# Dilated attention in one kernel of two blocks: query tiles by halves of classes, one product with the values per four tiles, and a gather moved to GpSimd

## The chip, the cores and the metric

The kernel runs as one launch on one core of a Trainium2 chip. The metric is the device time of that launch in microseconds (us), as the median of several runs. TensorE (PE in the profile, its weight loads PEld), VectorE (DVE), ScalarE (ACT), GpSimd (POOL) and SyncE (SP, which issues all DMAs) each work through a queue of their own in order and wait for one another by semaphores.

## The reference

Two transformer blocks on 1024 tokens of width 1024, float32. The change lies in the second block's dilated attention alone: eight heads of 64, each a mixture of three patterns (window 128 with dilation 1, 512 with 4, 2048 with 16). Cut to what matters:

```python
DIL_PATTERNS = ((128, 1), (512, 4), (2048, 16))

def dilated_branch(q, k, v, slopes, window, dilation):
    # query t attends to t + j*dilation for j in [-r, r], r = window // (2*dilation)
    ...
    s = jnp.einsum('bqnche,bnkche->bnchqk', qs, kw).astype(jnp.float32) * scale + bias
    s = jnp.where(mask, s, MASK_VALUE)
    m = jnp.max(s, axis=-1, keepdims=True)
    e = jnp.exp(s - m)
    l = jnp.sum(e, axis=-1, keepdims=True)
    o = jnp.einsum('bnchqk,bnkche->bnqche', e.astype(v.dtype), vw)
    ...

def dilated_attention(q, k, v, slopes):
    for window, dilation in DIL_PATTERNS:
        o, lse = dilated_branch(q, k, v, slopes, window, dilation)
        ...
    w = jax.nn.softmax(jnp.stack(lses, axis=0), axis=0)
    return jnp.sum(w[..., None] * jnp.stack(outs, axis=0), axis=0)
```

The kernel computes the three patterns as one softmax: the table `tab` holds slope times distance minus the logarithm of how many patterns contain the pair.

## The kernel before

Eight head pairs follow one another in the second block, four of the differential attention and then four of the dilated one (here pairs 0 to 3, two heads each; `dil_attend`). Tokens are sorted by their residue modulo 4, so there are four classes of 256 tokens. A query tile is half a class, 128 queries; tile `i` is half `i % 2` of class `i // 2`. A tile sees five blocks of 128 keys and, at the edge of its window, 16 more keys from each of three classes, together 688 scores per query and head.

Each tile has three steps, and `pipeline` sets their order:

```python
yield A(0)
yield A(1)
for i in range(n):
    if i + 2 < n:
        yield A(i + 2)
    if i + 2 == n:
        yield None
    if i:
        yield C(i - 1)
    yield B(i)
yield C(n - 1)
```

- A (scores): for each head four matmuls into two PSUM banks (L1267, L1269), two reductions on VectorE that add the table and take the minimum (L1272), the exponential on ScalarE (L1275). The result is `N`, 128 x 688.
- B (transposes): VectorE collects the 3 x 16 more keys of each head into `more` (L1290); eleven transposes on TensorE (four and four in L1294, one of each head in L1300, `more` in L1301); four copies out of PSUM, which the helper `evac` gives to ScalarE (L630) and VectorE (L632) by turns. So the first head's four blocks go to ScalarE, the second's to VectorE, and of the third bank the two single blocks go to ScalarE and the more keys to VectorE (the narrow copy, 96 x 128).
- C (product with the values): ten matmuls with 64 weight columns, one per block and head, and 128 columns of data (L1318), and one for the more keys of both heads (L1319). The output bank is filled by four tiles and then copied by ScalarE (L1322).

`bank()` takes the next of eight PSUM banks; `slot()` takes one of 40 general SBUF buffers. While the tiles of a pair run, `merge` puts pieces of the next pair's key projection between the steps, by cost numbers that each step returns (A 1160, B 1199, C 1561) and the ratio 0.27895. At the `None` the tiles pause, the projection runs to its end, and the remaining steps C(5), B(6), C(6), B(7), C(7) are the five `t` in a string that orders the way to the next pair:

```python
"fqfqqqtNftNtfvNvtvtNveNzzzzx"
```

`q`, `v` and `z` are half pieces of projections (twelve matmuls of 512 columns, L112 to L114), `N` the steps of the norms of the next keys and queries (sums over heads L255, their transposes L264, a reciprocal square root in thirteen small VectorE operations up to L246, rows out by a transpose L271 and by DMA), `f` and `e` the finish of an earlier pair (L1148, L1158 on VectorE, `rows_out` L271). For the last pair there is no next one: GpSimd splits rows of the next weight (`wo`, L118 and L121), ScalarE and GpSimd split the finished outputs (`yt`, L120 and L121), and after C(6) `pair_last` needs the sums of all eight tiles (L1380 on VectorE, L271 on TensorE) before B(7) and C(7).

Of the kernel before, what the change touches and what calls it, by code (L numbers as in the profile page):

```python
# [9 lines left out]
F32 = mybir.dt.float32  # L10
# [3 lines left out]
AF = mybir.ActivationFunctionType  # L14
# [52 lines left out]
class Kern:  # L67
# [593 lines left out]
    def ssd_chunks(self, g, st):  # L661
        nc, te, V, G = self.nc, self.nc.tensor, self.nc.vector, self.nc.gpsimd
# [42 lines left out]
        def prep(c):  # L705
            c0 = 16 + 128 * c
            cols = slice(c0, c0 + 128)
            ab = self.slot("ab", w=1024)
            nc.sync.dma_start(out=ab, in_=self.d_acs[c, hs].rearrange("h l -> (h l)").partition_broadcast(128))
            xdt, xdd, bt = tokens(c + 1, c0, 128)  # L710
            ps = self.bank()
            te.matmul(ps[:, :128], st["B"][:, cols], st["C"][:, cols])
            cbm = self.sm.tile([128, 128], F32, tag="cbm", name="cbm", bufs=2)
            V.tensor_tensor(out=cbm, in0=self.U, in1=ps[:, :128], op=ALU.mult)
            E = self.ph.tile([128, 520], F32, tag="E", name="E", bufs=2)
            for e in range(2):
# [12 lines left out]
            return ab, E, xdt, xdd, bt  # L729
# [520 lines left out]
    def dil_attend(self, p, st):  # L1250
        nc, te, V = self.nc, self.nc.tensor, self.nc.vector
        bias, k = st["bias"], st["k"]
        y = st["y"] = self.slot("yb", w=T)
        Ns, PTs, O = {}, {}, [None]

        def A(i):
            d = dil_tile(i)
            own = d["own"]
            n0, n1 = own.stop - own.start, d["nrest"]
            Ns[i] = []  # L1260
            for j in range(2):
                N = self.slot("N", w=T)
                mn = self.sm.tile([128, 3], F32, tag="mn", name="mn", bufs=4)
                S = self.bank(), self.bank()
                q = st["q"][j][:, i * 128:(i + 1) * 128]
# [9 lines left out]
                nc.scalar.activation(out=N[:, :688], in_=N[:, :688], func=AF.Exp, scale=-1.0, bias=mn[:, 1:2],  # L1275
                                     accum_out=self.lall[:, 4 + 2 * p + j, i:i + 1])
                Ns[i].append(N)
            return 8 * 145

        def B(i):  # L1280
            d = dil_tile(i)
            if i == 0:
                st["vx"] = next(st["vx"])
            big, small = self.slot("pt", w=1024), self.slot("pt", w=512)
            more = self.sm.tile([128, 128], F32, tag="cbm", name="more", bufs=2)[:, :96]
            for j in range(2):
                N = Ns[i][j]
                x = N[:, 256:688] if d["a"] == 0 else N[:, 0:432]
                e = slice(128, 144) if d["a"] == 0 else slice(0, 16)
                V.tensor_copy(out=more[:, 48 * j:48 * j + 48].rearrange("p (c e) -> p c e", e=16),  # L1290
                              in_=x.rearrange("p (c e) -> p c e", e=144)[:, :, e])
                ps = self.bank()
                for b, (_, c) in enumerate(d["blocks"][:4]):
                    te.transpose(ps[:, b * 128:(b + 1) * 128], N[:, c:c + 128], self.ident)  # L1294
                self.evac(big[:, j * 512:(j + 1) * 512], ps)
                ps = None
            ps = self.bank()
            c = d["blocks"][4][1]
            for j in range(2):
                te.transpose(ps[:, j * 128:(j + 1) * 128], Ns[i][j][:, c:c + 128], self.ident)  # L1300
            te.transpose(ps[:96, 256:384], more, self.ident)  # L1301
            self.evac(small[:, :256], ps[:, :256])
            self.evac(small[:96, 256:384], ps[:96, 256:384])
            PTs[i] = big, small
            del Ns[i]
            return 11 * 109

        def C(i):
            d = dil_tile(i)
            big, small = PTs.pop(i)  # L1310
            if i % 4 == 0:
                O[0] = self.bank()
            q = slice((i % 4) * 128, (i % 4 + 1) * 128)
            for b in range(5):
                for j in range(2):
                    c = slice(64 * j, 64 * j + 64)
                    x = big[:, j * 512 + b * 128:j * 512 + (b + 1) * 128] if b < 4 else small[:, j * 128:(j + 1) * 128]
                    te.matmul(O[0][c, q], st["v"][:, d["blocks"][b][0], c], x, start=b == 0, stop=False)  # L1318
            te.matmul(O[0][:, q], st["vx"][:96, i * 128:(i + 1) * 128], small[:96, 256:384], start=False, stop=True)  # L1319
            if i % 4 == 3:  # L1320
                g = i // 4
                nc.scalar.activation(out=by_class(y)[:, 2 * g:2 * g + 2], in_=O[0].rearrange("p (r s) -> p r s", r=2),  # L1322
                                     func=AF.Copy)
            return 5 * 269 + 216

        yield from self.pipeline(8, A, B, C)

# [486 lines left out]
```

## Time and profile before

| | |
|---|---|
| time, median of 3 runs (lowest to highest) | 2732.16 us (2728.64 to 2733.09) |
| the profiled execution: its time, its span | 2729.51 us, 2727.7 us |
| busy over the span: PE, PEld | 2659.8 us (98%), 2232.2 us (82%) |
| busy over the span: DVE, ACT, POOL | 1372.3 us, 1165.6 us, 684.5 us |
| mean granted TensorE clock | 0.994 of full speed |
| dilated stage, 2194 to 2513 us: PE, DVE, ACT, POOL busy | 294.5, 170.7, 159.7, 75.1 of 319 us |

The span is the time from the first to the last instruction; the execution's own time is 1.8 us longer. Busy times are sums over instructions. Those of PE are modelled to each matmul's end and overlap, so from one matmul's start to the next one's is the better measure of its price. A clock of 1.00 is the upper of TensorE's two levels (2.4 GHz), 0.50 the lower (1.2 GHz).

### The profile page before, as it was taken

To read this page: it belongs to the slowest core of one execution; us is meant where nothing else is said; L and a number is where in the kernel's file an instruction comes from. 1 tells how busy PE (TensorE), PEld (TensorE's weight loads), DVE (VectorE), ACT (ScalarE), POOL (GpSimd) and SP (SyncE) were. 2 spreads that over 40 slices of the span, in tenths; PEclk is the share of its full clock that TensorE was granted. 3 is DMA by queue.
4 is the path that set the end of the run, shared out by engine and by line. 5 is a ranking of instruction groups with operands and counts; after the bars stand their busy time and mean duration, and the time that the engine had idled before them with its cause. 6 is when DMAs were issued, how large, how long until landed. Compare 5 with 4: busy or idle time off the path is not lost. (4 is left out here: it accounts for less than half of the span.)

```text
span 2727.7 us, 38674 instructions
## 1 busy us (share of the span) xinstructions
PE 2659.8 (98%) x14925; PEld 2232.2 (82%) x14925; DVE 1372.3 (50%) x2761; ACT 1165.6 (43%) x2080; POOL 684.5 (25%) x764
## 2 busy tenths in 40 slices
PE   8999999999999999999999999999999999998999
PEld 6888888888989889889877887878877877777877
DVE  5433322233574573654756777444654555446332
ACT  5554444445343433443432123445644555445331
POOL 1112121111243342342432333111111121204321
PEclk9999999999999999999999999999999999998999
DMA  3122222221123123122168653340222223324422
GB/s 131 58 64 72 78 79 71 78 64 62 39 88 114 55 78 116 55 103 91 55 207 279 205 182 131 128 121 30 72 70 70 79 94 94 86 72 146 160 65 70
DMA packets 85464, 266.87 MB, mean 98 GB/s; under 512 B 10880, under 2 KB 12032, under 8 KB 84256
## 3 DMA queue, kind: packets, MB, share of 16 engines
q1 hardware_dynamic: 85280, 264.40, 30.3%
q8 instruction: 117, 1.92, 0.3%
q14 instruction: 67, 0.55, 0.1%
HBM read 205.57 MB, written 33.49 MB: 88 GB/s over the span
## 5 line engine op out<-in xcount | busy, mean ns | idle before, releaser
L121 POOL TENSOR_TENSOR wlo<-wraw,whi 128x1024 fp32r<-128x1024 f32 (+2 forms) x168 | 374.4, 2232 | 1288.7 <-ACT whi L120 1077.8
L112 PE MATMUL bank<-uh,whi 128*128 128x512 f32 (+4 forms) x1752 | 625.8, 357 | 0.1
L114 PE MATMUL bank<-uh,wlo 128*128 128x512 f32 (+4 forms) x1752 | 618.8, 353 | 0.1
L113 PE MATMUL bank<-ul,whi 128*128 128x512 f32 (+4 forms) x1752 | 618.5, 353 | 0.0
L114 PEld LDWEIGHTS bank<-uh,wlo 128*128 128x128 f32 (+1 forms) x1752 | 327.9, 187 | 35.4 <-POOL wlo L121 0.5
L112 PEld LDWEIGHTS bank<-uh,whi 128*128 128x128 f32 (+1 forms) x1752 | 328.3, 187 | 34.3 <-issue 1.1
L113 PEld LDWEIGHTS bank<-ul,whi 128*128 128x128 f32 (+1 forms) x1752 | 328.2, 187 | 32.3
L112 PE MATMUL bank<-u,whi 128*128 128x512 f32 x512 | 207.8, 406 | 0.7 <-ACT pr L935 0.7
L113 PE MATMUL bank<-u,whi 128*128 128x512 f32 x512 | 203.6, 398 | 0.0
L114 PE MATMUL bank<-u,wlo 128*128 128x512 f32 x512 | 203.3, 397 | 0.0
L120 ACT ACTIVATE whi<-wraw 128x1024 fp32r<-128x1024 f32 (+2 forms) x169 | 155.3, 926 | 20.5 <-DMA wraw<-in_w_pa_dram 18.2
L630 ACT ACTIVATE pt<-bank 128x512 f32<-128x512 f32 (+1 forms) x320 | 143.0, 509 | 44.8 <-PE bank L624 38.1
L114 PE MATMUL bank<-yh,wlo 128*128 128x512 f32 x384 | 152.5, 397 | 1.0 <-POOL wlo L121 0.8
L112 PE MATMUL bank<-yh,whi 128*128 128x512 f32 x384 | 152.3, 397 | 0.9 <-ACT whi L120 0.9
L113 PE MATMUL bank<-yl,whi 128*128 128x512 f32 x384 | 151.9, 395 | 0.0
L647 DVE SCALAR_TENSOR_TENSOR acc<-raw,cwh,acc 128x1040 f32<-128x1040 f32 x72 | 93.7, 1302 | 109.5 <-ACT acc L644 107.8
L573 ACT ACTIVATE N<-N,mn 128x272 f32<-128x272 f32 (+7 forms) x128 | 100.3, 786 | 45.2 <-DVE mn L570 44.0
L114 PEld LDWEIGHTS bank<-u,wlo 128*128 128x128 f32 x512 | 97.2, 190 | 23.2
L112 PEld LDWEIGHTS bank<-u,whi 128*128 128x128 f32 x512 | 97.8, 191 | 22.3 <-ACT pr L935 1.1
L113 PEld LDWEIGHTS bank<-u,whi 128*128 128x128 f32 x512 | 97.6, 191 | 20.7
L121 POOL TENSOR_TENSOR wo<-wl,wo 128x512 fp32r<-128x512 f32 x52 | 73.4, 1425 | 157.8 <-ACT wo L120 150.6
L624 PE MATMUL bank<-cm,N 128*128 128x128 f32 x832 | 106.9, 273 | 0.0
(326 smaller groups left out, 4961.5 us busy)
## 6 DMA issues: line engine op xcount, KB each, us to landing
wraw<-in_w_in_dram SPq DMA_DIRECT2D x120, 512.0 KB, 4.1
gt<-d_gate SPq DMA_DIRECT2D x48, 512.0 KB, 5.7
ab<-d_acs SPq DMA_DIRECT2D x32, 512.0 KB, 3.5
qs<-qt SPq DMA_DIRECT2D x48, 256.0 KB, 2.9
wl<-in_w_out_dram SPq DMA_DIRECT2D x48, 256.0 KB, 5.4
tab<-in_tab_dram SPq DMA_DIRECT2D x8, 1056.0 KB, 5.9
cb<-d_csp SPq DMA_DIRECT2D x16, 520.0 KB, 7.6
d_gate<-gt SPq DMA_DIRECT2D x16, 512.0 KB, 2.9
```

The costliest lines, as they stand in the source:

```text
L112: te.matmul(ps, lh, rh, start=start, stop=False)
L113: te.matmul(ps, lh, rl, start=False, stop=False)
L114: te.matmul(ps, ll, rh, start=False, stop=stop)
L120: self.nc.scalar.activation(out=hi, in_=src, func=AF.Copy)
L121: (self.nc.vector if vector else self.nc.gpsimd).tensor_tensor(out=lo, in0=src, in1=hi.bitcast(F32), op=ALU.subtract)
L573: nc.scalar.activation(out=N[:, :W], in_=N[:, :W], func=AF.Exp, scale=-1.0, bias=mn[:, n - 1:n], accum_out=self.lall[:, 2 * p + j, i:i + 1])
L624: nc.tensor.transpose(ps[:, b * 128:(b + 1) * 128], N[:, c:c + 128], self.ident)
L630: self.nc.scalar.activation(out=out, in_=ps, func=AF.Copy)
L647: V.scalar_tensor_tensor(out=acc[:, :L], in0=raw[:, k:k + L], scalar=w(k), in1=acc[:, :L], op0=ALU.mult, op1=ALU.add)
```

## The change

- The tiles run in the order 0, 2, 4, 6, 1, 3, 5, 7: first the first halves of all classes, then the second halves. The four tiles of a group share four blocks of keys (the same half of every class); each has one block of its own besides (the other half of its class).
- C does nothing for three tiles and then the product of four: eight matmuls of 512 columns of data, eight of 128 for the own blocks, and eight of 128 for the more keys, now per head with 64 weight columns. The output bank is taken only there. C returns 0 or 5300 as its cost.
- The transposed blocks of a group stand in two tiles of 4 x 512 (`pt`), one for each head, with two general buffers beside them.
- The more keys are gathered by GpSimd at the end of A (L1283) in place of VectorE in B (L1290); their buffers go from two to four.

```diff
-            cbm = self.sm.tile([128, 128], F32, tag="cbm", name="cbm", bufs=2)
+            cbm = self.sm.tile([128, 128], F32, tag="cbm", name="cbm", bufs=4)
...
+        order = [0, 2, 4, 6, 1, 3, 5, 7]
         def A(i):
-            d = dil_tile(i)
+            t, d = order[i], dil_tile(order[i])
...
+            Xs[i] = self.sm.tile([128, 128], F32, tag="cbm", name="more", bufs=4)[:, :96]
...
+                nc.gpsimd.tensor_copy(out=Xs[i][:, 48 * j:48 * j + 48].rearrange("p (c e) -> p c e", e=16),
+                                      in_=x.rearrange("p (c e) -> p c e", e=144)[:, :, e])
             return 8 * 145
         def B(i):
...
-            big, small = self.slot("pt", w=1024), self.slot("pt", w=512)
+            if r == 0:
+                PTs[a] = ([self.ph.tile([128, 4, 512], F32, tag="pt", name="pt", bufs=2) for _ in range(2)],
+                          self.slot("pt", w=1024), self.slot("pt", w=512))
+            pt, own, more = PTs[a]
+            q = slice(128 * r, 128 * r + 128)
+            blocks = sorted(d["blocks"], key=lambda x: (x[0] % 2 != a, x[0]))
             for j in range(2):
-                V.tensor_copy(out=more[:, 48 * j:48 * j + 48].rearrange("p (c e) -> p c e", e=16),
-                              in_=x.rearrange("p (c e) -> p c e", e=144)[:, :, e])
...
-                self.evac(big[:, j * 512:(j + 1) * 512], ps)
+                self.evac(pt[j][:, :, q], ps.rearrange("p (b c) -> p b c", c=128))
...
-            self.evac(small[:, :256], ps[:, :256])
-            self.evac(small[:96, 256:384], ps[:96, 256:384])
+            self.evac(own.rearrange("p (j c) -> p j c", j=2)[:, :, q], ps[:, :256].rearrange("p (j c) -> p j c", j=2))
+            self.evac(more[:96, q], ps[:96, 256:384])
         def C(i):
...
-            for b in range(5):
-                for j in range(2):
-                    te.matmul(O[0][c, q], st["v"][:, d["blocks"][b][0], c], x, start=b == 0, stop=False)
-            te.matmul(O[0][:, q], st["vx"][:96, i * 128:(i + 1) * 128], small[:96, 256:384], start=False, stop=True)
...
-            return 5 * 269 + 216
+            if i % 4 != 3:
+                return 0
+            a = order[i] % 2
+            pt, own, more = PTs.pop(a)
+            O = self.bank()
+            for c in range(4):
+                for j in range(2):
+                    te.matmul(O[h], st["v"][:, 2 * c + a, h], pt[j][:, c], start=c == 0, stop=False)
+            for r in range(4):
+                for j in range(2):
+                    te.matmul(O[h, q], st["v"][:, 2 * r + 1 - a, h], own[:, j * 512 + 128 * r:j * 512 + 128 * r + 128],
+                              start=False, stop=False)
+            for r in range(4):
+                for j in range(2):
+                    te.matmul(O[64 * j:64 * j + 64, q], st["vx"][:96, t * 128 + 64 * j:t * 128 + 64 * j + 64], more[:96, q],
+                              start=False, stop=r == 3)
+            nc.scalar.activation(out=by_class(y)[:, :, 128 * a:128 * a + 128], in_=O.rearrange("p (r s) -> p r s", r=4),
+                                 func=AF.Copy)
+            return 5300
```

Three places show how the queues change. First TensorE, the norms on the way from pair 1 to pair 2 (`sums` are the sums over heads, `u` and `whi` a projection). Before:

```order
L1301 MATMUL bank<-cm,more 96x128
L264 MATMUL bank<-cm,sums_20281 128x128 x4
L1318 MATMUL bank<-pt_20283,vtok_19710 64x128 x8
L1318 MATMUL bank<-pt_20284,vtok_19710 64x128 x2
L1319 MATMUL bank<-pt_20284,vx_19837 128x128
L112 MATMUL bank<-u_1111_15416,whi_20205 128x512
```

With the change:

```order
L255 MATMUL bank<-qr_20122,w_152 32x512 x2
L1303 MATMUL bank<-cm,N_19979 128x128 x4
L1303 MATMUL bank<-cm,N_19991 128x128 x4
L1309 MATMUL bank<-cm,N_19979 128x128
L1309 MATMUL bank<-cm,N_19991 128x128
L1310 MATMUL bank<-cm,more 96x128
L264 MATMUL bank<-cm,sums_20192 128x128 x4
L112 MATMUL bank<-u_1111_15416,whi_20127 128x512
```

The product C(6) has gone from between the sums' transposes L264 and the half piece of projection after which L271 stands; C(5) has gone from before L255 likewise.

Second VectorE in pair 1, around the finish of pair 0 (L1158, `yb` is pair 0's output). Before:

```order
L1272 ISA N_19941,mn<-tab,bank,mn 128x288
L1272 ISA mn 128x1
L1158 TENSOR_TENSOR yb_18891<-yb_18891,rb_19636 128x4x256
L1290 COPY more<-N_19815 128x48
L1290 COPY more<-N_19826 128x48
L632 COPY pt_19979<-bank 128x512
L632 COPY pt_19980<-bank 96x128
L1272 ISA N_20002,mn<-tab,bank 128x400
```

With the change:

```order
L1275 ISA N_19889,mn<-tab,bank,mn 128x432
L1275 ISA mn 128x1
L632 COPY pt<-bank 128x4x128
L632 COPY pt_19814<-bank 96x128
L1158 TENSOR_TENSOR yb_18891<-yb_18891,rb_19588 128x4x256
L1275 ISA N_19936,mn<-tab,bank 128x400
```

It stood behind the reductions of A(4) and ahead of the copies of B(1); now it stands behind the copies of B(2) and ahead of the reductions of A(5).

Third TensorE at the end of pair 3 (`lall` are the sums of all tiles, `yt` and `wo` the product that follows the attention). Before:

```order
L1318 MATMUL bank<-pt_21857,vtok_21344 64x128 x8
L1318 MATMUL bank<-pt_21858,vtok_21344 64x128 x2
L1319 MATMUL bank<-pt_21858,vx_21464 128x128
L271 MATMUL bank<-cm,lall 16x128
L1294 MATMUL bank<-cm,N_21763 128x128 x4
L1294 MATMUL bank<-cm,N_21774 128x128 x4
L1300 MATMUL bank<-cm,N_21763 128x128
L1300 MATMUL bank<-cm,N_21774 128x128
L1301 MATMUL bank<-cm,more 96x128
L1318 MATMUL bank<-pt_21900,vtok_21344 64x128 x8
L1318 MATMUL bank<-pt_21901,vtok_21344 64x128 x2
L1319 MATMUL bank<-pt_21901,vx_21464 128x128
```

With the change:

```order
L1310 MATMUL bank<-cm,more 96x128
L271 MATMUL bank<-cm,lall 16x128
L1303 MATMUL bank<-cm,N_21599 128x128 x4
L1303 MATMUL bank<-cm,N_21611 128x128 x4
L1309 MATMUL bank<-cm,N_21599 128x128
L1309 MATMUL bank<-cm,N_21611 128x128
L1310 MATMUL bank<-cm,more 96x128
L1325 MATMUL bank<-pt,vtok_21200 64x512 x8
L1330 MATMUL bank<-pt_21578,vtok_21200 64x128 x8
L1336 MATMUL bank<-pt_21579,vx_21329 64x128 x8
```

The product ahead of L271 has gone, and the one at the end is that of four tiles.

## Rows read from the trace of the kernel before

**Rows 1.** Windows, the dilated stage: length; busy us (instructions) of PE, PEld, DVE, ACT, POOL; clock.
```profile
2194.00:2513.00 319.00, 294.49 (x1995) 245.35 (x1996) 170.73 (x476) 159.72 (x283) 75.11 (x116) 0.96 0.30 91
```

**Rows 2.** Groups by line, dilated stage: count, busy us, mean ns, idle before.
```profile
L1290 DVE COPY more<-N 128x48 f32<-128x48 f32 x64 | 9.7, 193 | 0.0
...
L1301 PE MATMUL bank<-cm,more 128*96 128x128 f32 x32 | 9.1, 286 | 9.9 <-DVE more L1290 9.9
```

**Rows 3.** Timeline of DVE and of ACT, one tile's step in pair 3.
```profile
2478.10 0.56 DVE L1272 CUSTOM_DVE_ANT_0 N<-tab,bank 128x400 f32<-128x400 f32 x1
...
2482.54 0.56 DVE L1272 CUSTOM_DVE_ANT_0 N<-tab,bank 128x400 f32<-128x400 f32 x1
...
2480.58 0.87 ACT L1275 ACTIVATE N<-N,mn 128x688 f32<-128x688 f32 x1 [0.26 <-DVE mn L1272]
...
2481.45 0.85 ACT L630 ACTIVATE pt<-bank 128x512 f32<-128x512 f32 x2
```

**Rows 4.** Timeline of PE, one tile's product in pair 0: start us, us, instruction.
```profile
2209.88 1.31 PE L1318 MATMUL bank<-pt,vtok 128*64 128x128 f32 x20
...
2211.44 1.04 PE L1294 MATMUL bank<-cm,N 128*128 128x128 f32 x8
```

**Rows 5.** Timeline of PE, first block's attention, products over 512 columns.
```profile
101.32 2.85 PE L604 MATMUL bank<-pt,vtok 128*64 128x512 f32 x16 [0.36 <-ACT pt L630]
104.10 1.16 PE L607 MATMUL bank<-pm,vm 128*128 128x128 f32 x8
```

**Rows 6.** Timeline of POOL: copies of 48 columns in the dilated stage.
```profile
2289.74 0.37 POOL L1233 COPY vg<-vT 128x48 f32<-128x48 f32 x2
```

**Rows 7.** Timeline of PE, tiles 0 to 5 of pairs 0 and 1: first and last transposes.
```profile
2205.04 1.04 PE L1294 MATMUL bank<-cm,N 128*128 128x128 f32 x8
...
2236.78 0.31 PE L1301 MATMUL bank<-cm,more 128*96 128x128 f32 x1
...
2297.84 1.04 PE L1294 MATMUL bank<-cm,N 128*128 128x128 f32 x8
...
2327.31 0.27 PE L1301 MATMUL bank<-cm,more 128*96 128x128 f32 x1
```

**Rows 8.** Timeline of PE and DVE in pair 1: half a projection, scores; copy, finish.
```profile
2306.58 0.39 PE L112 MATMUL bank<-u,whi 128*128 128x512 f32 x1
...
2309.15 0.40 PE L114 MATMUL bank<-u,wlo 128*128 128x512 f32 x1
...
2316.29 0.37 PE L1267 MATMUL bank<-qs,qs 128*128 128x256 f32 x1
...
2317.74 1.31 PE L1318 MATMUL bank<-pt,vtok 128*64 128x128 f32 x20
...
2301.83 0.29 DVE L632 COPY pt<-bank 96x128 f32<-96x128 f32 x1 [0.23 <-ACT pt L630]
...
2309.08 2.11 DVE L1158 TENSOR_TENSOR yb<-yb,rb 128x1024 f32<-128x1024 f32 x1
```

**Rows 9.** Timeline of PE and ACT, the norms between pairs 0 and 1.
```profile
2250.99 1.31 PE L1318 MATMUL bank<-pt,vtok 128*64 128x128 f32 x20
...
2260.82 0.28 PE L271 MATMUL bank<-cm,rsv 128*32 128x128 f32 x1 [0.76 <-DVE rsv L246]
...
2251.59 0.59 ACT L1042 ACTIVATE qr<-bank 128x512 f32<-128x512 f32 x1
```

**Rows 10.** Timeline of ACT and PE, the end of pair 3.
```profile
2502.72 0.87 ACT L1275 ACTIVATE N<-N,mn 128x688 f32<-128x688 f32 x1 [0.19 <-issue]
...
2504.84 2.71 ACT L120 ACTIVATE yt<-y 128x512 fp32r<-128x512 f32 x5
...
2513.09 0.48 PE L112 MATMUL bank<-wo,yt 128*128 128x512 f32 x1
```

**Rows 11.** Timeline of PE in pair 3, and windows of PE alone: busy us, clock.
```profile
2492.30 0.45 PE L1301 MATMUL bank<-cm,more 128*96 128x128 f32 x1 [2.60 <-DVE more L1290]
...
2495.00:2500.00 5.00, 5.00 (x39) 0.67 0.80 284
```

More of the change, by code (lines that the diff above doesn't have):

```diff
@@ L1253, in dil_attend @@
         y = st["y"] = self.slot("yb", w=T)
-        Ns, PTs, O = {}, {}, [None]
+        Ns, Xs, PTs = {}, {}, {}
+        order = [0, 2, 4, 6, 1, 3, 5, 7]
         def A(i):
-            d = dil_tile(i)
+            t, d = order[i], dil_tile(order[i])
             own = d["own"]
@@ L1264, in A @@
                 S = self.bank(), self.bank()
-                q = st["q"][j][:, i * 128:(i + 1) * 128]
+                q = st["q"][j][:, t * 128:(t + 1) * 128]
                 for v in range(2):
@@ L1275, in A @@
                 nc.scalar.activation(out=N[:, :688], in_=N[:, :688], func=AF.Exp, scale=-1.0, bias=mn[:, 1:2],
-                                     accum_out=self.lall[:, 4 + 2 * p + j, i:i + 1])
+                                     accum_out=self.lall[:, 4 + 2 * p + j, t:t + 1])
                 Ns[i].append(N)
+                x = N[:, 256:688] if d["a"] == 0 else N[:, 0:432]
+                e = slice(128, 144) if d["a"] == 0 else slice(0, 16)
+                nc.gpsimd.tensor_copy(out=Xs[i][:, 48 * j:48 * j + 48].rearrange("p (c e) -> p c e", e=16),
+                                      in_=x.rearrange("p (c e) -> p c e", e=144)[:, :, e])
@@ L1278, in A @@
             return 8 * 145
         def B(i):
-            d = dil_tile(i)
+            t, d = order[i], dil_tile(order[i])
+            r, a = t // 2, t % 2
             if i == 0:
                 st["vx"] = next(st["vx"])
-            big, small = self.slot("pt", w=1024), self.slot("pt", w=512)
-            more = self.sm.tile([128, 128], F32, tag="cbm", name="more", bufs=2)[:, :96]
-            for j in range(2):
-                N = Ns[i][j]
-                x = N[:, 256:688] if d["a"] == 0 else N[:, 0:432]
-                e = slice(128, 144) if d["a"] == 0 else slice(0, 16)
-                V.tensor_copy(out=more[:, 48 * j:48 * j + 48].rearrange("p (c e) -> p c e", e=16),
-                              in_=x.rearrange("p (c e) -> p c e", e=144)[:, :, e])
+            if r == 0:
+                PTs[a] = ([self.ph.tile([128, 4, 512], F32, tag="pt", name="pt", bufs=2) for _ in range(2)],
+                          self.slot("pt", w=1024), self.slot("pt", w=512))
@@ L1292, in B @@
+            pt, own, more = PTs[a]
+            q = slice(128 * r, 128 * r + 128)
+            blocks = sorted(d["blocks"], key=lambda x: (x[0] % 2 != a, x[0]))
+            for j in range(2):
                 ps = self.bank()
-                for b, (_, c) in enumerate(d["blocks"][:4]):
-                    te.transpose(ps[:, b * 128:(b + 1) * 128], N[:, c:c + 128], self.ident)
-                self.evac(big[:, j * 512:(j + 1) * 512], ps)
+                for b, (_, c) in enumerate(blocks[:4]):
+                    te.transpose(ps[:, b * 128:(b + 1) * 128], Ns[i][j][:, c:c + 128], self.ident)
+                self.evac(pt[j][:, :, q], ps.rearrange("p (b c) -> p b c", c=128))
@@ L1296, in B @@
                 ps = None
             ps = self.bank()
-            c = d["blocks"][4][1]
+            c = blocks[4][1]
             for j in range(2):
                 te.transpose(ps[:, j * 128:(j + 1) * 128], Ns[i][j][:, c:c + 128], self.ident)
-            te.transpose(ps[:96, 256:384], more, self.ident)
-            self.evac(small[:, :256], ps[:, :256])
-            self.evac(small[:96, 256:384], ps[:96, 256:384])
-            PTs[i] = big, small
+            te.transpose(ps[:96, 256:384], Xs.pop(i), self.ident)
@@ L1308, in C @@
         def C(i):
[L1309 to L1313, printed above, removed]
-            for b in range(5):
-                for j in range(2):
-                    c = slice(64 * j, 64 * j + 64)
-                    x = big[:, j * 512 + b * 128:j * 512 + (b + 1) * 128] if b < 4 else small[:, j * 128:(j + 1) * 128]
-                    te.matmul(O[0][c, q], st["v"][:, d["blocks"][b][0], c], x, start=b == 0, stop=False)
-            te.matmul(O[0][:, q], st["vx"][:96, i * 128:(i + 1) * 128], small[:96, 256:384], start=False, stop=True)
[L1320 to L1323, printed above, removed]
-            return 5 * 269 + 216
+            if i % 4 != 3:
[4 more added lines that the diff above has]
+            for c in range(4):
+                for j in range(2):
+                    h = slice(64 * j, 64 * j + 64)
+                    te.matmul(O[h], st["v"][:, 2 * c + a, h], pt[j][:, c], start=c == 0, stop=False)
+            for r in range(4):
+                q = slice(128 * r, 128 * r + 128)
+                for j in range(2):
+                    h = slice(64 * j, 64 * j + 64)
+                    te.matmul(O[h, q], st["v"][:, 2 * r + 1 - a, h], own[:, j * 512 + 128 * r:j * 512 + 128 * r + 128],
+                              start=False, stop=False)
+            for r in range(4):
+                q = slice(128 * r, 128 * r + 128)
+                t = 2 * r + a
+                for j in range(2):
[4 more added lines that the diff above has]
+            return 5300
         yield from self.pipeline(8, A, B, C)
```

## The prediction, made before the change was run

> **What bounds the kernel now.** I read the windows first. In the dilated stage TensorE is busy 294.5 of 319 us and no other engine more than 171 [rows 1]: TensorE sets the pace, so work taken from it counts, as long as nothing else comes up close behind. The mean clock of 0.96 says that some of this stage ran at the lower level. The groups come second: TensorE's only large wait that the change touches is the 9.9 us in front of L1301, for VectorE's copies of the more keys, 64 of 193 ns [rows 2].
>
> The timelines decide the case, because the three steps of a tile are also a loop between VectorE and ScalarE. Take one round [rows 3]. The four reductions of a tile start at 2478.10 and the last exponential can start at 2480.58. ScalarE runs it (0.87 and some 0.1 to read its sum) and only then its two copies of the tile two places earlier; the narrow copy on VectorE waits for the second of them, as it did for 0.23 in pair 1 [rows 8], and the next reductions stand behind the narrow copy, at 2482.54. A round is 4.44 us, 4.42 over two; the copies take about 0.85 and 0.2 of it. The product and the gather are no part of this round. TensorE needs per tile 1.4 for the scores (2316.29 to 2317.74, less the gap) [rows 8], 1.1 for the transposes (eight in 0.87, three more at the same pace) and 1.56 for the product [rows 4], 4.1 together. So the bound of today has a second one 0.3 us behind it, and only half pieces of projections (2.8, twelve matmuls from 2306.58 to 2309.15 and one more step [rows 8]) put TensorE clearly above.
>
> **The change part by part.** *Product.* Before, a tile takes 1.56 us: ten matmuls in 1.24 (0.124 each) and the joint one in 0.32 [rows 4]; eight tiles make 12.5. After, eight matmuls of 512 columns, which took 2.78 in the first block (101.32 to 104.10, same 64 weight columns) [rows 5], and sixteen of 128 columns at 0.124, 1.98: 4.77 per four tiles, 9.5 per pair. The sixteen might cost as the joint one does (0.32 for two heads, so 0.16 each for those of the more keys): then 5.05. TensorE's work falls by 2.4 to 3.0 us per pair.
>
> *Gather.* 9.7 us leave VectorE and the 9.9 us of waits leave TensorE [rows 2]. On GpSimd a copy of 48 columns took 0.37 for two that overlap [rows 6], so about 0.2 each, an estimate; GpSimd is busy 75 of 319 us [rows 1], and the result is wanted two rounds (8.9 us) later. I cost it at nothing. The cover is those two rounds; without it one late gather costs what it is late, as L1290 does now.
>
> *The inside of a pair.* What is left per tile on TensorE is 2.5 us against a round of 4.42, so most of what is saved becomes a wait for VectorE and ScalarE, unless a projection fills it. I sum the stretch from the first transposes of B(0) to the end of B(5): now 31.8 us in pair 0 and 29.6 in pair 1, whose form pair 2 has too [rows 7]. After: the narrow copy of tile 0 ends 4.3 us after B(0)'s start (2297.84 to 2302.12 [rows 7, 8]), 4.0 without the two copies in front; three rounds to tile 3's, 13.3; C(3) can start 0.4 before that narrow copy ends, and takes 4.8; then B(4) 1.1, half a projection 2.8, A(7) 1.4 and B(5) 1.1. That is 28.1. In pairs 1 and 2 the finish of an earlier pair (L1158, 2.1 [rows 8]) now stands in the round before A(5), where before it stood beside work of TensorE: 30.2. In pair 0 L1158 has no place there, and I allow 1.1, an estimate, for small operations of the norms on VectorE: 29.2. Against before: -2.6, +0.6, +0.6, sum -1.4.
>
> *The way to the next pair, three times.* C(6) stood between the sums' transposes and L271, and TensorE waited there 0.76 for the thirteen small operations [rows 9]; without the product it comes 1.57 earlier and waits that much longer. C(5) stood before L255. Its input, L1042, ends at 2252.18, while the projection is done at 2250.99 [rows 9]; three quarters of L255 can run first, so 0.45 is waited. The work itself is +0.1 (two products of 1.56 gone, the last one 3.2 longer). The copy out of C(7)'s bank still stands ahead of the next pair's copies on ScalarE, so the wait at A(0) moves along with it at no cost. 2.1 each, 6.3 in all.
>
> *Last pair.* No projection fills it. Eight rounds now run unhindered by the waits at L1301, but C(3) with B(4) holds a round up by 2.2 (5.9 on TensorE against 3.7 of reductions and exponential). I put the last exponential's end at 2501.3, against 2503.6 now [rows 10]. Behind it stands on ScalarE: one split `yt` 0.6, two copies 0.85, six splits 3.3 (five took 2.71 [rows 10]), two copies 0.86, then, by the sizes of the parts above, the narrow copy, reciprocal and L271 0.8, B(7) 1.1, its copies 0.9 and all of C(7), 4.8: 13.2, so 2514.5, where `wo`'s product starts at 2513.09 now [rows 10]. That is +1.4. The finished outputs load behind L1158, which is now later, and TensorE idles some 6 us here, after which the clock may fall; bounds 0 to +7, I take +2.5.
>
> Sum: -1.4 + 6.3 + 2.5 = +7.4 on the profiled execution's 2729.5, 2736.9. The median of the runs stands 2.65 above that execution, so I forecast **2739** for the median. No change can be told from 0.2%, 5.5 us, either way.
>
> **The clock.** A wait of 2.60 at L1301 is followed by scores and a product at half speed: the next 5 us stand in a window of 0.67 [rows 11]. That is the only kind of place where the clock falls in the stage: behind TensorE's idle time. In the sum I leave the number of such falls as it is.
>
> The Trainium skill, "TensorE: Matmul & The Clock Gate", section "HAM oscillation — how this bites in real kernels", tells of the same thing as a pattern: where short groups of matmuls alternate with waits for data, each group begins at the lower clock. By that rule a tile's 2.5 us of work between waits could start cold again and again. The trace agrees as far as the fall behind the 2.60 goes; no row of it shows waits that follow one another as closely as the changed kernel's would.
>
> **Rivals.** *A, TensorE stays the bound and all of the saving arrives.* For it: 98% busy over the span, and 9.9 us of waits that truly go. Then each of the three stretches gains three us of product (five of 1.56 become one of 4.8) and 2.0 of wait, -15; the last pair 3.0 and 2.6, -5.6; the transitions stay +6.3: -14.3, a time of 2718. Faster than before. Against it: the round of 4.44, which contains none of what is removed. It decides if ScalarE's copies need not wait behind the exponential, so that a round falls below 3.5.
>
> *B, a wash.* Half of the gain of A and no clock loss at the end: the first rounds of each pair start sooner because TensorE runs ahead, and the projection is pulled into the waits. About -1 to +2 in sum, 2729 to 2735.
>
> *C, more falls of the clock.* New waits: 2.3 at L271 three times, some 3 before C(3) four times, 6 at the end. A fall took C from 1.31 to about twice that; 5 us at 0.67 lose 1.7, and a whole product of 4.8 at half speed would lose 4.8. Six or seven falls more are +12: 2751.
>
> *D, the gather is late.* GpSimd's queue holds splits in the last pair and gathers elsewhere; VectorE's L1158 took 2.1 beside them. If a gather comes behind such work by more than two rounds, L1310 waits as L1301 did: the 9.9 return, and the time is 2745 or so. Against it: 8.9 us of slack.
>
> The Trainium skill, "SBUF — State Buffer", section "Who interferes with whom", has VectorE's two-port copies and GpSimd lock one another out of a shared pair of ports. By it the gathers could hold up VectorE's copies inside the round; no row of this trace has a gather on GpSimd to show it.
>
> **How the numbers follow.** The forecast (slower, 2735 to 2746) 0.34; A 0.20; B 0.30; C 0.11; D 0.05. The range goes from A's 2718 to just below C's 2751, 2750: half of A, most of C and little of D lie outside, under 2 in 10. Faster by over 0.2% (below 2726.7): A and a little of B, 0.22. Within 0.2% (to 2737.6): most of B and the lower edge of the forecast, 0.34. Slower: 0.44.
>
> **What would show it.** L1301's successor L1310 should have no wait for GpSimd, and L1290 no successor on VectorE; C should take 4.7 to 5.1. The first reductions of successive tiles should follow at 4.4 us; at 3.5 or less, the inside of a pair is wrong and A is right. TensorE should wait about 2.3 before L271 between pairs, and B(0) to B(5) should take 29 to 30 us. The last exponential should end near 2501 after the start, `wo`'s product start at 2514 to 2520. More stretches below 0.9 in clock than today would mean C. I am wrong if the rounds shorten, or if the projection is moved so that it covers the new waits.

## The result, and the profile after

The changed kernel takes 2755.97 us (median of 4 runs, 2753.61 to 2758.07) against 2731.63 for the kernel before: a ratio of 1.009, 95% interval 1.0073 to 1.0108. It is slower by 24 us; forecast were 7.4, with 2750 as the upper end. The profiled execution of the change took 2756.43 us, its span 2754.6.

The windows of the dilated stage after (columns as in [rows 1]), the whole stage and then pair 1 from its first scores to those of pair 2; the last line is the same pair of the kernel before:

```profile
2198.00:2540.00 342.00, 304.59 (x1677) 230.15 (x1678) 163.96 (x414) 158.98 (x284) 89.24 (x180) 0.94 0.28 87
2292.90:2391.20 98.30, 89.19 (x470) 66.99 (x471) 44.96 (x108) 44.16 (x75) 17.66 (x38) 0.93 0.27 82
2286.33:2376.79 90.46, 84.63 (x550) 70.16 (x551) 46.78 (x124) 44.51 (x75) 14.16 (x22) 0.96 0.30 89
```

The same pair took 90.46 before, at a clock of 0.96. TensorE now has 470 matmul rows there and before 550, and yet it is busy longer, 89.2 us against 84.6, in part because more of its matmuls run at the lower clock (the twelve behind L271 below take 4.43 in place of 2.87); 9 us of the pair it is idle, before 6. In the groups by line, the wait in front of the transposes of the more keys has gone, 9.9 us before [rows 2]:

```profile
L1283 POOL COPY more<-N 128x48 f32<-128x48 f32 x64 | 16.1, 254 | 114.1 <-ACT N L1278 113.7
L1310 PE MATMUL bank<-cm,more 128*96 128x128 f32 x32 | 8.9, 277 | 0.0
```

By places, from the timelines of TensorE of both kernels (us, after minus before, spans of the two profiles):

| place | forecast | measured |
|---|---|---|
| ahead of the stage, where the two programs are alike | 0 | +3.75 |
| A(0) to B(0), pairs 0, 1, 2 | 0 | -0.88, -0.13, +1.04 |
| B(0) to the end of B(5), pairs 0, 1, 2 | -2.6, +0.6, +0.6 | -1.27, +3.09, +3.14 |
| end of B(5) to the next A(0), three times | +2.1 each | +4.93, +4.94, +5.05 |
| last pair, A(0) to the product with `wo` | +2.5 | +3.09 |
| behind it | 0 | +0.16 |
| sum | +7.4 | +26.9 |

The first line is no part of the change: over all profiles of this study the last projection ahead of the stage starts between 2177.30 and 2181.05, and these two happen to be the ends. It is why the profiles differ by 26.9 and the medians by 24.3.

Three places on TensorE tell most. The timeline between pairs 0 and 1, where C(6) stood before (compare L271 in [rows 9]), and below it the window of TensorE behind the wait (us, busy, clock):

```profile
2256.08 0.60 PE L264 MATMUL bank<-cm,sums 128*128 128x128 f32 x4
...
2262.03 0.28 PE L271 MATMUL bank<-cm,rsv 128*32 128x128 f32 x1 [2.56 <-DVE rsv L246]
2262.07 0.56 PE L112 MATMUL bank<-u,whi 128*128 128x512 f32 x1
...
2266.50 1.04 PE L1303 MATMUL bank<-cm,N 128*128 128x128 f32 x8
```

```profile
2262.00:2266.50 4.50, 4.47 (x13) 0.62 0.24 62
```

The wait is 2.56 in place of 0.76, and the half piece behind it takes 4.43 (2262.07 to 2266.50) where the same twelve matmuls took 2.87 before. The clock of 0.62 in that window is the reason: a wait of 2.6 costs 1.6 more behind itself.

The first product of four tiles in pair 1, with the waits ahead of it:

```profile
2320.07 0.40 PE L1272 MATMUL bank<-qs,qs 128*128 128x288 f32 x1 [1.20 <-DVE mn L1275]
...
2323.35 5.35 PE L1325 MATMUL bank<-pt,vtok 128*64 128x512 f32 x16 [1.58 <-ACT pt L630]
...
2330.38 0.88 PE L1303 MATMUL bank<-cm,N 128*128 128x128 f32 x6
```

And windows of TensorE ahead of it and over it:

```profile
2318.00:2324.00 6.00, 3.08 (x17) 0.98 0.65 224
2324.00:2331.00 7.00, 7.00 (x54) 0.77 0.10 40
```

TensorE is busy half of the 6 us ahead, and then the product takes 7.03 (2323.35 to 2330.38) at a clock of 0.77. In pair 0 it took 5.33, behind a wait of the same length:

```profile
2226.58 3.65 PE L1325 MATMUL bank<-pt,vtok 128*64 128x512 f32 x16 [1.58 <-ACT pt L630]
2230.07 1.04 PE L1330 MATMUL bank<-pt,vtok 128*64 128x128 f32 x16
2230.94 1.04 PE L1336 MATMUL bank<-pt,vx 96*64 96x128 f32 x16
2231.91 0.33 PE L1303 MATMUL bank<-cm,N 128*128 128x128 f32 x1
```

And the sequence of VectorE and ScalarE in pair 1, where one tile's first reduction follows the last one's after 4.39 us, behind the narrow copy, which waits for ScalarE:

```profile
2308.20 0.41 DVE L1275 CUSTOM_DVE_ANT_0 N<-tab,bank 128x256 f32<-128x256 f32 x1
...
2312.38 0.29 DVE L632 COPY pt<-bank 96x128 f32<-96x128 f32 x1 [1.18 <-ACT pt L630]
2312.59 0.41 DVE L1275 CUSTOM_DVE_ANT_0 N<-tab,bank 128x256 f32<-128x256 f32 x1
...
2310.63 0.87 ACT L1278 ACTIVATE N<-N,mn 128x688 f32<-128x688 f32 x1 [0.20 <-DVE mn L1275]
...
2311.50 0.85 ACT L630 ACTIVATE pt<-bank 128x512 f32<-128x512 f32 x2
```

### The profile page after: what moved, and what is told of

Same layout as the page of the kernel before. It is cut to its first block, busy times and chain, and to the rows that moved or that the text cites. A ratio compares the mean times of both kernels' runs of the same rounds, so it can differ in the third digit from the quotient of the medians.

```text
span 2754.6 us, 38015 instructions
## 1 busy us (share of the span) xinstructions
PE 2669.5 (97%) x14605; PEld 2216.8 (80%) x14605; DVE 1363.3 (49%) x2697; ACT 1165.9 (42%) x2080; POOL 699.2 (25%) x828
## 5 line engine op out<-in xcount | busy, mean ns | idle before, releaser
L112 PEld LDWEIGHTS bank<-u,whi 128*128 128x128 f32 x512 | 98.7, 193 | 23.2 <-ACT pr L935 1.1
```

The costliest lines, as they stand in the source:

```text
L112: te.matmul(ps, lh, rh, start=start, stop=False)
```

## The experiments

Two theories stood against each other. The first: inside a pair the round between VectorE and ScalarE sets the pace, and between pairs the products of tiles 5 and 6 had covered waits that now lie open, with falls of the clock behind them. The second: TensorE's work sets the pace, and the change lost because its work is dearer or because of the gather. Times are medians; the kernel before, run beside them, gave 2731.97 to 2732.55.

**e1, the gather alone** on the kernel before (order and products as before):

```diff
-                V.tensor_copy(out=more[:, 48 * j:48 * j + 48]...      # in B
+                nc.gpsimd.tensor_copy(out=Xs[i][:, 48 * j:48 * j + 48]...   # at the end of A
```

> The kernel before with nothing but the gather moved to GpSimd, at the end of the scores; order of tiles and products as before. The round theory (reductions on VectorE, exponential and two copies on ScalarE, narrow copy on VectorE: 4.4 us a tile, whatever TensorE does): the 9.9 us of waits in front of the transposes of the more keys go from TensorE, but only those that the round does not bring back count; 2724 to 2731 us. If TensorE's own work sets the pace, all of the 9.9 arrive and some falls of the clock go with them: 2716 to 2722. If the gather on GpSimd is what costs the change its time, this kernel is slower than before: 2740 or more.

2725.39, ratio 0.9977 (0.9967 to 0.9987): as the round theory has it. The gather is a gain of 6.6 us by itself, and the product by fours in the new order turns it into a loss of 24: it costs 31.

**e2, a cover ahead of L271**, one `v` moved in the order of the way to the next pair:

```diff
-          "fqfqqqtNftNtfvNvtvtNveNzzzzx")
+          "fqfqqqtNftNtfvvNtvtNveNzzzzx")
```

> The changed kernel with one half piece of the values' projection moved ahead of the norms' L271 on the way to each pair of the dilated attention, where the product of tile 6 stood before the change. If the loss there is lack of cover and the clock's fall behind the wait: L271 waits 0.3 or less in place of 2.5, the next half piece takes 2.9 in place of 4.4, four ways between pairs, of which three were long: 9 to 12 us less than the changed kernel, 2744 to 2747. If the time lies in TensorE's work itself: no difference that can be measured.

2744.33, ratio 1.0046 (1.0033 to 1.006): 11.6 us come back. The stretch from the end of B(5) to the next A(0) takes 49.9 in place of 54.2, three times, since the wait and the slower half piece behind it are both gone; the last pair took 2.5 more in this profile. On TensorE of this kernel L271 no longer waits:

```profile
2261.40 0.40 PE L112 MATMUL bank<-u,whi 128*128 128x512 f32 x1
2262.10 0.27 PE L271 MATMUL bank<-cm,rsv 128*32 128x128 f32 x1
```

**e3, transposes first**, the tiles' steps in another order on all engines:

```diff
-        yield from self.pipeline(8, A, B, C)
+        yield A(0)
+        yield A(1)
+        for i in range(8):
+            if i == 6:
+                yield None
+            if i:
+                yield C(i - 1)
+            yield B(i)
+            if i < 6:
+                yield A(i + 2)
+        yield C(7)
```

> The changed kernel with the transposes of tile i and their copies ahead of the scores of tile i+2, on all engines, so that ScalarE's copies no longer stand behind the exponential of the tile two places later. Round theory: reductions of successive tiles follow at 3.3 to 3.6 us in place of 4.4, a pair's tiles get 3 to 4 us shorter, and the product of the first four tiles starts without a fall of the clock: 2736 to 2746. If TensorE's work sets the pace: within 4 us of the changed kernel.

2741.42, ratio 1.0032 (1.002 to 1.0045). The time is what the theory named, but not for its reason. The timeline of VectorE in this kernel:

```profile
2304.98 0.56 DVE L1275 CUSTOM_DVE_ANT_0 N<-tab,bank 128x400 f32<-128x400 f32 x1
...
2309.16 0.29 DVE L632 COPY pt<-bank 96x128 f32<-96x128 f32 x1 [1.18 <-ACT pt L630]
2309.37 0.41 DVE L1275 CUSTOM_DVE_ANT_0 N<-tab,bank 128x256 f32<-128x256 f32 x1
```

The round is still 4.39: in a chain of A, B, A, B it makes no difference which is called first; ScalarE's copies stand behind the exponential before them either way. What was gained lies around it: one tile's scores go from ahead of the first transposes to a place behind them (A(0) to B(0) 0.8 to 1.3 shorter in pairs 0 and 1), and C(3) of pairs 1 and 2 ran in 5.33 in place of 7.03. Over its whole stage (331 us) the mean clock is 0.96, with the change 0.94 (of 342 us): by that some 7 us less are lost to the lower clock, an estimate, which is half of the gain.

**e4, the first group's product in parts**: the matmuls of 512 columns at C(3), the own blocks at C(5), the more keys and the copy out at C(6).

```diff
+        def C(i):
+            if i == 3:
+                blocks_part(0)
+                return 3500
+            if i == 5:
+                own_part(0)
+                return 900
+            if i == 6:
+                more_part(0)
+                return 900
...
```

> The changed kernel with the first group's product in three parts: the eight matmuls of 512 columns where the whole stood, the own blocks at the place of tile 5's product (ahead of L255) and the more keys at that of tile 6 (ahead of L271). The same work on TensorE. Theory of missing cover: each part of 0.87 us takes as much from the wait behind it, and leaves the place inside the tiles; 1.7 us a pair, three pairs, and the first clock falls shorter: 2747 to 2752. If the work's amount sets the time: no difference.

2742.49, ratio 1.0038 (1.0025 to 1.005): 13.5 us, more than the 4 to 9 expected. With the lower cost that C(3) returns, one half piece of projection also moves from ahead of A(7) to a place behind it. The parts cover what they should, and L271 has no wait at all, for a second reason, seen by laying VectorE and GpSimd of the changed kernel beside those of this one. The changed kernel:

```profile
2257.78 2.38 DVE L239 TENSOR_TENSOR rsa<-rsy 128x32 f32<-128x32 f32 x1
...
2257.69 2.43 POOL L121 TENSOR_TENSOR wlo<-wraw,whi 128x1024 fp32r<-128x1024 f32 x1 [11.65 <-ACT whi L120]
```

This kernel:

```profile
2260.51 0.19 DVE L239 TENSOR_TENSOR rsa<-rsy 128x32 f32<-128x32 f32 x1
...
2262.57 2.39 POOL L121 TENSOR_TENSOR wlo<-wraw,whi 128x1024 fp32r<-128x1024 f32 x1 [13.55 <-ACT whi L120]
```

One small operation of the norms takes 2.38 where a weight's split on GpSimd runs beside it, and 0.19 where the split comes later; here ScalarE's copy of the product stands ahead of the split's first half. The kernel before has the longer form too (2.35). So some 2.2 of the changed kernel's wait of 2.56 at L271 are this delay. It goes with the product in parts: in the five kernels that have it (e4, e5, e9, e13, e14) no operation of these norms is delayed, and in every other kernel of the study one of them takes 2.3 to 2.4 on each way between pairs. The part of the 13.5 that is due to this was not measured apart.

**e5, e4 and e3 together.**

> The changed kernel with both edits at once: the first group's product in three parts, and transposes ahead of the scores of two tiles later. If the two act on different losses (waits between pairs; rounds inside a pair), the gains of 13.5 and 14.5 us add up but for the product that fell to half clock, which both spare: 2730 to 2734. If both only spare the same falls of the clock: 2740.

2729.25, ratio 0.9993 (0.9984 to 1.0001): just below what was expected: the gains add up almost whole, to the time of the kernel before, and still 3.9 above the gather alone.

**e6, the gather alone with transposes first**, the edit of e3 on e1.

> The kernel with the gather on GpSimd alone and the old product, with the transposes of tile i ahead of the scores of tile i+2. Here TensorE works 4.1 us a tile, the round is 4.4. Round theory: the round falls to about 3.4, TensorE's 4.1 is what is left, 0.3 us a tile and the last pair's waits: 3 to 6 us less than the gather alone, 2719 to 2723. If the round binds only where the product has gone: the same as the gather alone, 2725.

2725.69, ratio 0.9977 (0.9968 to 0.9986): no gain, where the round theory had named 3 to 6 us. It agrees with what e3's rows say: this edit doesn't shorten the round.

**e7, the gather alone with the cover**, the edit of e2 on e1.

> The kernel with the gather on GpSimd alone and the old product, with a half piece of the values' projection moved ahead of L271 as before. L271 waits 0.6 to 0.8 there, four times, and no clock falls behind it: 2 to 3 us less, 2722 to 2724. If the wait is not on the path: the same, 2725.

2733.05, ratio 1.0003 (0.9995 to 1.0012): 7.7 slower than e1, a miss of sign. L271's wait went, but so did 2 us of lead: the norms end later by the half piece that now stands ahead of L271, and the next pair's scores wait for what hangs on them, 4.24 here, 2.07 in e1:

```profile
2290.25 0.67 PE L1268 MATMUL bank<-qs,qs 128*128 128x400 f32 x1 [4.24 <-ACT vtok L469]
```

In e2 the longer last product hid this; in pair 0, where nothing did, the wait is 4.3 there too. The clock is lower behind the longer waits: 0.95 over the whole stage, 0.98 in e1.

**e8, the last pair's splits later**: the splits `yt` behind L271 and the transposes of tile 7.

```diff
-        for _ in y2:
-            yield 700
+        self.y2_rest = y2
...
                 next(last)
+                next(a)
+                run(self.y2_rest)
                 run(a)
```

> The changed kernel with the splits of the finished outputs of the last pair issued behind the sums' transpose L271 and the transposes of tile 7, in place of ahead of the copies of tile 6. If the wait of 6.3 us at L271 in the last pair comes from these splits on ScalarE: that wait falls to 2 or 3, and 2 to 5 us are gained, the rest given back because the splits on GpSimd (1.28 each) are late for the product behind: 2751 to 2754. If the wait is for something else: 2756.

2752.46, ratio 1.0079 (1.0066 to 1.0091): 3.5 us, the size expected, but the runs of the two kernels overlap (2750.05 to 2757.26 here, 2753.61 to 2758.07 with the change), and the gain is not shown. In the profile the wait at L271 falls to 2.72, as named, and the last pair takes 47.18 in place of 49.88; what follows it takes 218.8 in place of 214.8. What the splits hold up in the changed kernel is seen on ScalarE, VectorE and TensorE, from the last exponential on:

```profile
2526.23 3.22 ACT L120 ACTIVATE yt<-y 128x512 fp32r<-128x512 f32 x6
2529.35 0.86 ACT L630 ACTIVATE pt<-bank 128x512 f32<-128x512 f32 x2
...
2530.24 0.29 DVE L632 COPY pt<-bank 96x128 f32<-96x128 f32 x1 [2.99 <-ACT pt L630]
...
2530.84 0.37 PE L271 MATMUL bank<-cm,lall 128*16 128x128 f32 x1 [6.32 <-DVE lall L1396]
```

**e9, e10, e11: e8's edit on e5, on e1 and on e6.**

> The changed kernel with all three edits: product of the first group in parts, transposes ahead of the scores of two tiles later, splits of the finished outputs behind the last pair's L271. The splits alone were worth 3.5 us on the changed kernel, and the wait at L271 is as long here (6.4): 2725 to 2727. If the product by fours, once its waits are covered, is the gain that its shorter work promises, it is below the old product with the gather alone, 2725.4; if the round and the waits still hold it, above.

> The gather on GpSimd alone, with the old product, and the splits of the finished outputs behind the last pair's L271. There TensorE waits 2.0 us for ScalarE's copies behind such splits and some 1.5 in the transposes of tile 6; the splits on GpSimd become late by 2 for the product that follows: 2723 to 2726.

> The gather alone with the old product, transposes ahead of the scores of two tiles later, and the splits behind the last pair's L271. With transposes first, pairs 0 to 2 came out equal or up to 1 us shorter and the last pair 3.1 longer, with a wait of 4.1 behind these splits: 2721 to 2724 if that wait goes, 2725 if it is only moved to the product behind.

2728.39 (ratio 0.9985, 0.9976 to 0.9994), 2730.5 (0.9991, 0.9982 to 1.0) and 2728.67 (0.9986, 0.9977 to 0.9994): 0.9 less (within the noise), 5.1 more and 3.0 more than without it; all three lie above what was named. The last pair does get shorter (in e10 42.32 from its A(0) to the product with `wo`, 44.46 in e1), but what follows takes 222.4 in place of 215.3, since that product now waits for the splits, and runs on at the lower clock behind the waits:

```profile
2510.81 0.49 PE L114 MATMUL bank<-wo,yt 128*128 128x512 f32 x1 [0.25 <-POOL yt L121]
2513.67 0.50 PE L112 MATMUL bank<-wo,yt 128*128 128x512 f32 x1 [2.37 <-ACT yt L120]
2515.02 0.80 PE L114 MATMUL bank<-wo,yt 128*128 128x512 f32 x1 [0.52 <-POOL yt L121]
```

**e12, the round broken**: since e3 had not touched the round, the narrow copy goes from VectorE to ScalarE, behind the copy of the same bank.

```diff
-            self.evac(more[:96, q], ps[:96, 256:384])
+            self.evac(more[:96, q], ps[:96, 256:384], act=True)
```

> The changed kernel with the narrow copy of the more keys (96 x 128) on ScalarE, behind the copy of the same bank, in place of VectorE: VectorE no longer waits for ScalarE before the next tile's reductions. Round theory: reductions of successive tiles follow at 3.0 to 3.5 us in place of 4.4, four rounds ahead of each first product, about 4 us a pair and as much in the last: 2740 to 2746. If something else holds the tiles at 4.4 (transposes first did not change it): the same as the changed kernel, 2756.

2735.43, ratio 1.0012 (1.0003 to 1.0021): 20.5 us for one copy of 0.2 us moved, more than expected. VectorE in pair 1 of this kernel:

```profile
2307.54 0.41 DVE L1275 CUSTOM_DVE_ANT_0 N<-tab,bank 128x256 f32<-128x256 f32 x1
...
2309.85 0.69 DVE L632 COPY pt<-bank 128x512 f32<-128x512 f32 x1
2310.45 0.41 DVE L1275 CUSTOM_DVE_ANT_0 N<-tab,bank 128x256 f32<-128x256 f32 x1
```

The round is 2.91 in place of 4.39, and no wait for ScalarE is left in it. That is below the 3.0 to 3.5 expected, and pairs 1 and 2 take 93.56 and 91.04 in place of 98.37 and 98.74, the last 44.77 in place of 49.88; pair 0 became 2.2 longer. The clock has a part in this: C(3) takes 5.33 in pairs 1 and 2, 7.03 with the change, and 7.03 in pair 0, 5.33 with the change. L271 still waits 2.2 to 2.3 here, three times, with a half piece of 4.3 to 4.4 behind it.

**e13, e14, e15: e12's edit on e4, on e5 and on e1.**

> The same narrow copy on ScalarE, together with the first group's product in three parts (2742.5 alone). If round and waits between pairs are separate losses, the two add up: 2727 to 2733; if the parts already spare what the round costs: 2740.

> Product in parts, transposes ahead of the scores of two tiles later (2729.3 together), and the narrow copy on ScalarE. Round theory: some 3 us a pair fewer, 2718 to 2723, and then the product by fours, with its waits covered, beats the old product with the gather alone (2725.4). If the round is not what holds it: 2729.

> The gather alone with the old product and the narrow copy on ScalarE. TensorE works 4.1 us a tile there and the round is 4.4, so of a shorter round only 0.3 a tile can arrive, most of it in the last pair: 2722 to 2725, against 2725.4 without.

2730.19 (0.9995, 0.9986 to 1.0004), 2715.89 (0.9941, 0.9928 to 0.9954) and 2721.79 (0.9961, 0.9948 to 0.9974): the first as expected, the others 2.1 and 0.2 below what was named. e14 is the fastest kernel of the study, 16.5 below the kernel before it was run with: with the waits between pairs covered and the round broken, the product by fours is 5.9 below the best that was run with the old product. That is not a comparison of the products alone. The old product with transposes first and the narrow copy on ScalarE was not run; without transposes first the product by fours is the slower one (e13 against e15, by 8.4). And e14 is free of the delay in the norms (e4): they end 1.0 ahead of L271, so with the 2.2 of the delay L271 would wait some 1.2, three times, an estimate. Pair 1 of e14 in a window, to be read beside that of the change:

```profile
2282.00:2368.00 86.00, 82.48 (x471) 64.88 (x471) 40.70 (x100) 45.47 (x83) 19.69 (x38) 0.98 0.31 93
```

## Why the prediction was wrong

- **The round: right.** 4.42 was forecast and some 4.4 is there; e12 shows that it set the pace inside the pair, and e3 and e6 that another order of the steps leaves it as it is. Rival A, all of the saving arriving, falls, and so does B, the wash: with the round standing, the product by fours gains nothing over the old one even with its waits covered (e5, 3.6 above e6, both with transposes first). B's sum does not follow from its own words either, half of A's 20.6 against the 6.3 being -4, but nothing hung on it.
- **The product: mis-sized**, 4.77 forecast, 5.33 measured at full clock (3.49 for the eight of 512 columns, 0.87 and 0.97 for the two times eight of 128, in the lines of pair 0 above). The step "eight matmuls of 512 columns, which took 2.78 in the first block" read [rows 5] wrongly: a grouped row bears the shape of its first instruction, and this one mixes four widths. The groups of the kernel before in that stretch, with the shapes kept apart:

```profile
L604 PE MATMUL bank<-pt,vtok 128*64 128x512 f32 x4 | 1.6, 618 | 0.4 <-ACT pt L630 0.4
L604 PE MATMUL bank<-pt,vtok 128*64 128x384 f32 x4 | 1.3, 486 | 0.0
L604 PE MATMUL bank<-pt,vtok 128*64 128x256 f32 x4 | 1.1, 379 | 0.0
L604 PE MATMUL bank<-pt,vtok 128*64 128x128 f32 x4 | 0.8, 272 | 0.0
```

  The eight cost 0.7 more, the sixteen 0.14 less; 0.56 a product, 4.5 us over eight. TensorE's saving is 1.8 per pair, not the 2.4 to 3.0 given.
- **The clock: the step that failed**, "in the sum I leave the number of such falls as it is", a term put at nothing without a reason. Each of the three waits at L271, forecast at 2.3 and measured at 2.5, was followed by a half piece at 4.26 to 4.43 in place of 2.87; C(3) took 7.03 in pairs 1 and 2, and the last product 6.37. Over the prices at full clock that is 4.5, 3.4 and 1.0: 9 us. The whole stage agrees: 0.94 of 342 us against 0.96 of 319 us is some 8 us more lost to the lower clock, an estimate from two rounded figures. This is rival C's mechanism, which had been given 0.11; its price of 12 was about right, but it was worked out as an alternative to the forecast, where it followed from the forecast's own waits. The Trainium skill, "TensorE: Matmul & The Clock Gate", section "HAM oscillation — how this bites in real kernels", says that groups of matmuls with long waits between them each begin at the lower clock. The trace agrees at these places: 0.62 behind the wait of 2.56, 0.77 in the product behind 6 us half idle. It does not hold at each place. Of twelve waits of 2.2 to 2.6 at L271 (the changed kernel, e3, e8, e12) eleven have a half piece of 4.2 to 4.4 behind them; the second in e3, of 2.52, has one of 2.85. Behind the 1.58 ahead of C(3) the product took 5.33 in pair 0 and 7.03 in pairs 1 and 2; in e8, whose edit touches the last pair alone, it took 5.33 in pair 1. What decides between the two is open.
- **The way to the next pair: the wait at L255 mis-sized.** L255 was to wait 0.45, three quarters of it running first; it takes 2.22 from its start to the next transposes, 1.00 before, so it costs 1.2 more. Three times 0.8 more than forecast. Little of it is idle time (0.19). Before, its eight matmuls run together in 1.00; now three quarters run first, in about as long, and the last quarter takes 0.97 by itself. The kernel before, then the changed one, between pairs 1 and 2:

```profile
2343.12 1.07 PE L255 MATMUL bank<-qr,w 128*32 128x512 f32 x8
2344.12 0.33 PE L1294 MATMUL bank<-cm,N 128*128 128x128 f32 x1
```

```profile
2350.94 1.06 PE L255 MATMUL bank<-qr,w 128*32 128x512 f32 x6
2352.19 1.04 PE L255 MATMUL bank<-qr,w 128*32 128x512 f32 x2 [0.19 <-ACT qr L1042]
2353.16 0.33 PE L1303 MATMUL bank<-cm,N 128*128 128x128 f32 x1
```

  The rest of that sum held: L271's wait, and C(7) moving A(0) along at no cost.
- **The last pair: right in sum** (+3.1, forecast +2.5), with the parts as described, ScalarE's splits ahead of the copies of tile 6 among them. The last exponential ends 35.0 behind A(0), as forecast; from there to `wo` it takes 14.9, forecast 13.2, and the last product, 6.37 for 4.8, makes up the difference.
- **The gather: right**, no wait is left at L1310. Rival D falls; e1 shows the gather as a gain.
- **The sum.** Product 4.5, clock 9.0 and L255 2.3 make 15.8; with the 7.4 forecast 23.2, against 23.0 measured inside the stage. That it closes so well is partly chance, since allowances of the forecast (1.1 in pair 0's stretch and in the last pair) stand in it for what is itemised here.

## What to carry to other kernels

Before work is taken from the busiest engine, find the round of the other engines that its steps close, and compare that with what will be left: here 2.5 us of TensorE against a round of 4.4, and the round hung on one copy of 0.2 us on the wrong engine. Work that is gathered into one place uncovers every wait that it used to stand in front of, and on TensorE an uncovered wait can be paid a second time in the clock behind it: 1.3 to 1.6 us behind waits of 2.2 to 2.6 at L271, in eleven places of twelve. The same edits are worth other amounts to a kernel whose engine is still full: the narrow copy gave 20.5 us to the changed kernel and 3.6 to the one with the old product (e15), transposes first gave that one nothing (e6), and the cover cost it 7.7 (e7). Such edits have to be tried with the change that they serve.

## What the runs showed of the hardware that was not expected

In these traces VectorE and GpSimd hold one another up in places: the instruction that starts second ends only when the other engine's has ended. Besides L239 (2.38 beside a split, 0.19 without, and so on all three ways between pairs of the changed kernel), one gather of 48 columns on GpSimd took 2 us longer while L1158 ran on VectorE; GpSimd, then VectorE, in pair 3 of the changed kernel:

```profile
2513.62 0.23 POOL L1283 COPY more<-N 128x48 f32<-128x48 f32 x1 [0.93 <-ACT N L1278]
...
2516.91 2.25 POOL L1283 COPY more<-N 128x48 f32<-128x48 f32 x2 [1.15 <-ACT N L1278]
...
2516.86 2.12 DVE L1158 TENSOR_TENSOR yb<-yb,rb 128x1024 f32<-128x1024 f32 x1
```

The Trainium skill, "SBUF — State Buffer", section "Who interferes with whom", has it so: an instruction of VectorE with two inputs in SBUF contends with one of GpSimd that reads there, and the one that comes second is blocked. Both cases here are of that kind. The prediction drew on the same section for VectorE's copies in the round. Those read PSUM, and none was held up: of the 64 in the changed kernel's stage 32 ran beside an instruction of GpSimd, and all took 0.69 or 0.29.
